# Five gate projections of a hybrid decoder layer, formed as block products by Strassen's scheme with tokens on the partitions

## The chip, the cores and the metric

The kernel runs on one core of a Trainium2 chip. It is one program: TensorE does the matrix products, VectorE and ScalarE the elementwise work, SyncE (SP) issues every DMA, GpSimd does next to nothing. The metric is the device time of one execution in microseconds, the median of three runs. Time before: 1664.78 us (1664.39 to 1664.81).

## What is computed

One layer, 512 tokens (S), width 2048 (D), float32:

```
h    = rmsnorm(x) * (1 + scale) + shift          # shift, scale, gate = silu(c) @ w_ada + b_ada
proj = h @ w_in                                  # 2048 x (768 + 512 + 64 + 6 * 2048)
q_lat, kv_lat, k_rope, z_mla, u, v, z_sgu, g_mla, g_sgu = split(proj)
y_mla = causal_attention(rmsnorm(q_lat) @ w_uq, rmsnorm(kv_lat) @ w_ukv, k_rope) * silu(z_mla)
mixed = tril(w_spatial) @ rmsnorm(v) + b_spatial # per group of 128 channels and chunk of 128 tokens
y_sgu = u * mixed * silu(z_sgu)
out   = rmsnorm(x + gate * ((sigmoid(g_mla) * y_mla + sigmoid(g_sgu) * y_sgu) @ w_out))
```

The five projections that only gate something (z_mla, g_mla, u, z_sgu, g_sgu; in the code z, g, u, s, t) are five products of 512 x 2048 by 2048 x 2048. They are the largest part of the arithmetic.

## The kernel before

**Precision.** Every large product is made of three: each operand is split into a high part in the matmul's float32r type and the low rest, and `mm3` (L133) adds high by high, high by low and low by high in one PSUM bank. Splitting takes a copy on ScalarE and a subtraction on VectorE (`hilo`, L138). Weights are split too: `Stream` (L53) brings a granule of 128 x 1024 numbers by DMA into one of three raw tiles (`dma_to`, L76), copies it to `whi` on ScalarE (L97), subtracts to `wlo` on VectorE (L98), and keeps two such pairs. `get` (L103) hands a granule to the matmuls and first emits the split of the next one and the DMAs behind it.

**Order.** The program runs under a manual schedule: each engine takes its instructions in the order in which the Python code emits them, and waits in place where an operand isn't ready. Small tasks are kept in two lists, `pend` (evacuations of PSUM) and `bg` (background), and a loop pops one between the matmuls of two granules. DMAs stand in one queue (SP) in the order of emission; `load_before` ties a load to the DMA of a granule.

**Stages.**
1. The adaLN products (dot products on VectorE, L125, rows of `wada`) beside the first 1024 columns of the projection (latents), then 640 more (the latent rest, and the last 128 columns of z, g and u). These 1664 columns are computed without the shift, whose share is added later: `shift_share` (L224) multiplies the raw weights, loaded a second time, with the shift on VectorE, `shift_bias` (L599) sums over the partitions.
2. The v columns (L466), tokens on the partitions: h is the stationary operand, 512, 384 or 320 columns of weights move. `evac_v` (L487) copies v into SBUF tiles `b0` to `b15`.
3. The gate stage (L749 to L827). For each of 15 heads (128 columns) and each of the five types: one PSUM bank, two granules, 8 chunks of 128 of the depth each, three matmuls a chunk: weights are stationary, 512 tokens of h move. Channels therefore lie on the partitions. `evac` (L693) multiplies the result into the tiles `g` and `b` of that head, with a sigmoid on ScalarE where it is a silu or a gate; these tiles stay in SBUF until the attention merges them. The last head's s and t follow (L814). Beside it run, from `bg` or at fixed places: the SGU mixing of each pair of groups (`sgu_prep`, `sgu_mix`, L649 to L690), the rotary tables (`rope_part`, L520, 34 small VectorE operations for each of four parts), 32 shares of the shift, and from head 8 on the scaling, squares, roots and norms of the latents (L612 to L717), their splitting (`lat_split`, L795) and the rotary key.
4. The attention, head by head (L1008): projections of q, k and v from the latents, scores, softmax, transposes, value product, merge with the gates.
5. The output projection, residual and final norm (L1068).

PSUM has eight banks, given out in turn by `bank` (L295).

## Time and profile before

| | |
|---|---|
| median of three runs | 1664.78 us |
| the profiled execution | 1664.88 us, span 1663.2 us, granted clock 0.999 |
| busy: TensorE, VectorE, ScalarE, GpSimd | 1651.6, 947.5, 583.3, 2.2 us |
| DMA | 228.6 MB, mean 137 GB/s |

By stages, from the windows of the trace (us):

| stretch | stage | TensorE | VectorE | ScalarE | DMA share |
|---|---|---|---|---|---|
| 0 to 101 | adaLN, first latents | 97.3 | 86.9 | 45.8 | 0.88 |
| 101 to 155 | 640 more columns | 54.0 | 50.6 | 18.5 | 0.84 |
| 155 to 337 | v | 182.0 | 95.8 | 61.8 | 0.55 |
| 337 to 788 | gates, heads 0 to 7, SGU, tables | 451.0 | 246.5 | 135.6 | 0.38 |
| 788 to 1201 | gates, heads 8 to 15, latents | 413.0 | 161.7 | 120.5 | 0.28 |
| 1201 to 1480 | attention | 278.9 | 223.8 | 148.5 | 0.20 |
| 1480 to 1663 | output | 175.3 | 82.2 | 52.8 | 0.38 |

How to read the rows shown below: a group of instructions gives line, engine, operation, what it writes and reads, shapes and count, then busy microseconds and the mean nanoseconds of one, then how long the engine was idle just before them and what it waited for. A row of the timeline gives start, duration, engine, line and operation. Matmuls overlap, so their spacing, not their duration, is the price. PE is TensorE, DVE VectorE, ACT ScalarE, SPq the queue of SP.

### The profile page before, as it was taken

The numbers are of one execution on the slowest core, as the hardware profiler recorded it, in microseconds if no ns is written. First come the engines' busy times: TensorE is split into PE (matmuls) and PEld (weight loads), VectorE is DVE, ScalarE is ACT, GpSimd is POOL, SyncE is SP. The second block draws the span as 40 slices with busy tenths as digits, with TensorE's granted clock in tenths as the row PEclk, the third lists the DMA queues.
The fourth block names the chain that finished last, engine by engine and source line by source line (L and its number), as shares of the span: only waits on it lengthen the run. The fifth ranks groups of instructions, "written<-read, shape, count | busy, mean of one in ns | idle before, by whom it ended". The sixth has DMA issues, their size and how long they took to land.

```text
span 1663.2 us, 20082 instructions
## 1 busy us (share of the span) xinstructions
PE 1651.6 (99%) x8024; PEld 1406.1 (85%) x8024; DVE 947.5 (57%) x1456; ACT 583.3 (35%) x967; POOL 2.2 (0%) x11
## 2 busy tenths in 40 slices
PE   9999999999999999999999999999999999999998
PEld 7888889988888888888888888888898888888887
DVE  8988646365665644444443533323578778874453
ACT  4343333234223322221223322222455555542332
POOL 0000000000000000000000000000000000000000
PEclk9999999999999999999999999999999999999999
DMA  9878557344444333322222222232311221126332
GB/s 379 346 295 303 193 211 269 101 151 143 142 152 132 120 137 127 123 102 89 98 92 102 89 101 100 90 102 81 96 61 58 63 75 55 61 77 253 127 101 101
DMA packets 64508, 228.63 MB, mean 137 GB/s; under 512 B 7304, under 2 KB 9376, under 8 KB 57632
## 3 DMA queue, kind: packets, MB, share of 16 engines
q1 hardware_dynamic: 64416, 227.37, 38.7%
q8 instruction: 62, 1.02, 0.2%
q14 instruction: 30, 0.25, 0.0%
HBM read 223.14 MB, written 4.20 MB: 137 GB/s over the span
## 4 chain that ended last, share of the span: by engine, by line
PE 98%; DMA 1%; DVE 0%; ACT 0%; issue 0%; SPq 0%; DVEq 0%
PE ps L135 32%; PE ps L134 32%; PE ps L136 32%; PE ps L947 1%; PE ps L675 1%; PE ps L910 1%; PE ps L911 1%; DMA wraw<-in_w 1%; PE ps L676 0%; DMA wada<-in_c 0%; PE ps L606 0%; DVE wlo L98 0%; ACT whi L97 0%; PE ps L446 0%; DVE wada L122 0%
## 5 line engine op out<-in xcount | busy, mean ns | idle before, releaser
L98 DVE TENSOR_TENSOR wlo<-wraw,whi 128x1024 fp32r<-128x1024 f32 (+3 forms) x304 | 339.0, 1115 | 577.4 <-ACT whi L97 566.4
L134 PE MATMUL ps<-hh,whi 128*128 128x512 f32 x1640 | 641.6, 391 | 0.2 <-ACT hh L389 0.2
L135 PE MATMUL ps<-hl,whi 128*128 128x512 f32 x1640 | 638.5, 389 | 0.8 <-DVE hl L125 0.8
L136 PE MATMUL ps<-hh,wlo 128*128 128x512 f32 x1640 | 638.4, 389 | 0.0
L97 ACT CAST whi<-wraw 128x1024 fp32r<-128x1024 f32 (+3 forms) x304 | 293.7, 966 | 801.6 <-PE ps L135 561.0
L136 PEld LDWEIGHTS ps<-hh,wlo 128*128 128x128 f32 x1640 | 307.8, 188 | 64.5 <-DVE wlo L98 0.2
L135 PEld LDWEIGHTS ps<-hl,whi 128*128 128x128 f32 x1640 | 308.0, 188 | 64.0 <-DVE hl L125 1.1
L134 PEld LDWEIGHTS ps<-hh,whi 128*128 128x128 f32 x1640 | 307.9, 188 | 63.7 <-ACT hh L389 0.6
L134 PE MATMUL ps<-whi,hh 128*128 128x512 f32 (+3 forms) x448 | 148.9, 332 | 0.0
L135 PE MATMUL ps<-wlo,hh 128*128 128x512 f32 (+3 forms) x448 | 148.6, 332 | 0.1
L136 PE MATMUL ps<-whi,hl 128*128 128x512 f32 (+3 forms) x448 | 148.5, 332 | 0.0
L125 DVE SCALAR_TENSOR_TENSOR wada<-wada,cact 128x2048 f32<-128x2048 f32 x47 | 107.2, 2281 | 1.2 <-DMA wada<-in_wada 1.2
L135 PEld LDWEIGHTS ps<-wlo,hh 128*128 128x128 f32 x448 | 84.6, 189 | 5.4 <-DVE wlo L98 0.4
L136 PEld LDWEIGHTS ps<-whi,hl 128*128 128x128 f32 x448 | 84.6, 189 | 5.0
L134 PEld LDWEIGHTS ps<-whi,hh 128*128 128x128 f32 x448 | 84.6, 189 | 5.0
L134 PE MATMUL ps<-whi,b 128*128 128x512 f32 (+1 forms) x212 | 81.8, 386 | 0.0
L135 PE MATMUL ps<-wlo,b 128*128 128x512 f32 (+1 forms) x212 | 81.6, 385 | 0.0
L136 PE MATMUL ps<-whi,g 128*128 128x512 f32 (+1 forms) x212 | 81.6, 385 | 0.0
L134 PEld LDWEIGHTS ps<-whi,b 128*128 128x128 f32 x212 | 39.8, 188 | 7.9
L135 PEld LDWEIGHTS ps<-wlo,b 128*128 128x128 f32 x212 | 39.8, 188 | 7.9
L136 PEld LDWEIGHTS ps<-whi,g 128*128 128x128 f32 x212 | 39.8, 188 | 7.9
L139 ACT CAST lat<-ps 128x512 fp32r<-128x512 f32 (+1 forms) x64 | 35.4, 570 | 13.4 <-PE ps L136 13.3
(229 smaller groups left out, 1340.8 us busy)
## 6 DMA issues: line engine op xcount, KB each, us to landing
wraw<-in_wh SPq DMA_DIRECT2D x150, 512.0 KB, 3.3
wada<-in_wada SPq DMA_DIRECT2D x47, 1024.0 KB, 5.9
wraw<-in_w SPq DMA_DIRECT2D x32, 512.0 KB, 3.5
wraw<-in_wo SPq DMA_DIRECT2D x32, 512.0 KB, 3.3
wraw<-in_w SPq DMA_DIRECT2D x32, 320.0 KB, 2.9
wraw<-in_wv SPq DMA_DIRECT2D x16, 512.0 KB, 3.2
wraw<-in_wv SPq DMA_DIRECT2D x16, 384.0 KB, 3.3
wraw<-in_wq SPq DMA_DIRECT2D x16, 384.0 KB, 2.9
```

The costliest lines, as they stand in the source:

```text
L97: self.nc.scalar.copy(hi[:, :n], raw[:, :n])
L98: self.nc.vector.tensor_tensor(out=lo[:, :n], in0=raw[:, :n], in1=hi[:, :n].bitcast(F32), op=ALU.subtract)
L125: DVE.scalar_tensor_tensor(out=out, in0=in0, scalar=scalar, in1=in1, op0=op0, op1=op1, **kw)
L134: PE.matmul(ps, ah, bh, start=start, stop=False)
L135: PE.matmul(ps, ah, bl, start=False, stop=False)
L136: PE.matmul(ps, al, bh, start=False, stop=stop)
L139: ACT.copy(hi, src)
L675: PE.matmul(ps[:, n2], vh[:, n, :], whl[:, q], start=True, stop=False)
L910: PE.matmul(ps, q2[:, q], krh[:, :n], start=False, stop=False)
L911: PE.matmul(ps, q2[:, q], krl[:, :n], start=False, stop=True)
L947: PE.transpose(ps[:, o:o + P], pr_[i][:, j * P:(j + 1) * P], ident)
```

## The change

The five projections are cut into ten blocks of twice 512 columns (one of twice 320; z, g and u lack their last 128 columns, as before). In a block the 512 tokens, the depth of 2048 and the columns are halved: h becomes four quarters of 256 x 1024, the weights four of 1024 x 512. Strassen's scheme (in Winograd's form) makes the four quarters of the result from seven products of quarters. Each product has four granules ("items" in the code) of 256 rows of the depth, 12 matmuls each: two chunks, two token tiles, three matmuls. h is stationary, weights move, so tokens lie on the partitions.

Four sums of quarters of h are formed once and kept split: S1, S2 and S4 in new tiles during the v columns, S3 in place of a quarter of h that is no longer needed. The sums of weight quarters are formed anew in each block on VectorE before they are split: a running sum T in the order of the products P1, P6, P2 with P7, P3, P5, P4. Products accumulate in PSUM (banks `y` and `z`, two token tiles each); three intermediate results are copied to SBUF by ScalarE, and the four quarters of the result come from PSUM and these copies.

There is no room to keep results in SBUF, and they have tokens on the partitions. So `gates` loads the step before (z for g, mixed v for u, and so on) from DRAM, multiplies, and stores again; after g and t the tile is transposed on TensorE (`turned`) and stored, and the attention loads it head by head (`fetch`). v, the mixed v, the latents and the rotary key go through DRAM too. The SGU mixing now has the spatial weights stationary and four chunks of v moving, with the bias added by ScalarE. Latent scaling is done during the v columns. `Stream` takes raw tiles and pairs from lists that grow and shrink (three pairs and up to four raw tiles in this stage), may need two loads for a granule or none, and `get` now splits two granules ahead.

The diff, cut to its core:

```diff
+BLOCKS = (
+    ((("z", 0, 512),), (("z", 512, 512),)),
+    ((("z", 1536, 384), ("g", 1024, 128)), (("z", 1024, 512),)),
+    ((("g", 0, 512),), (("g", 512, 512),)),
+    ((("u", 0, 512),), (("u", 512, 512),)),
+    ((("g", 1664, 256), ("u", 1664, 256)), (("g", 1152, 512),)),
+    ((("u", 1024, 320),), (("u", 1344, 320),)),
+    ((("s", 0, 512),), (("s", 512, 512),)),
+    ((("t", 0, 512),), (("t", 512, 512),)),
+    ((("s", 1024, 512),), (("s", 1536, 512),)),
+    ((("t", 1024, 512),), (("t", 1536, 512),)),
+)
...
+            src = form(raws) if form is not None else raws[0][:, :n]
             if to is not None:
                 hi, lo = to()
             else:
-                hi = self.pool.tile([P, GW], F32R, tag="whi", name=f"whi{k}", bufs=self.hl_bufs)
-                lo = self.pool.tile([P, GW], F32R, tag="wlo", name=f"wlo{k}", bufs=self.hl_bufs)
-            self.nc.scalar.copy(hi[:, :n], raw[:, :n])
-            self.nc.vector.tensor_tensor(out=lo[:, :n], in0=raw[:, :n], in1=hi[:, :n].bitcast(F32), op=ALU.subtract)
+                pool, tag = self.parts[self.next_part]
+                self.next_part = (self.next_part + 1) % len(self.parts)
+                hi = pool.tile([P, GW], F32R, tag=tag + "h", name=f"{tag}h_{k}")
+                lo = pool.tile([P, GW], F32R, tag=tag + "l", name=f"{tag}l_{k}")
+            self.nc.scalar.copy(hi[:, :n], src)
+            self.nc.vector.tensor_tensor(out=lo[:, :n], in0=src, in1=hi[:, :n].bitcast(F32), op=ALU.subtract)
             self.hl[k] = (hi, lo)
-        for consume, raw in later:
+            if after is not None:
+                after(raws)
+            if not keep:
+                self.free(k)
+            if frees is not None:
+                self.free(frees)
...
-        self.dma_to(self.n_split - 1 + self.raw_bufs)
+        self.dma_to(self.n_split + 6)
...
+                elif whole:
+                    n = w - (P if c0 + w == D else 0)
+                    src = wh[h:h + n // P, t, kh][:, :, i * 256:(i + 1) * 256].rearrange("h p w -> p h w")
+                    loads.append((lambda x, o=o, n=n: x[:, 2 * o:2 * (o + n)].rearrange("p (h w) -> p h w", w=256), src))
...
+        def first(raws, b=b, i=None, n=n):
+            if T[i] is None or T[i][0] != b:
+                T[i] = (b, nt(c1[0].p, [P, GW], F32, f"T{i}"))
+            tt(T[i][1][:, :n], raws[0][:, :n], raws[1][:, :n], ALU.add)
+        def t_of(raws, i, n=n):
+            return T[i][1][:, :n]
+        def t_add(raws, i, n=n):
+            t = T[i][1][:, :n]
+            tt(t, t, raws[0][:, :n], ALU.add)
+            return t
+        def both(raws, n=n):
+            t = raws[0][:, :n]
+            tt(t, t, raws[1][:, :n], ALU.add)
+            return t
+        kept = {}
+        def hold(raws, i, n=n, kept=kept):
+            kept[i] = raws[0][:, :n]
+            return t_add(raws, i, n)
+        seq = [(1, i) for i in range(4)] + [(6, i) for i in range(4)]
+        seq += [(2, 0), (7, 0), (2, 1), (7, 1), (2, 2), (2, 3), (7, 2), (7, 3)]
+        seq += [(p, i) for p in (3, 5, 4) for i in range(4)]
+        for p, i in seq:
+            if p == 1:
+                e = ws.add((w(0, 0, i), w(0, 1, i)), n, after=lambda raws, f=first, i=i: f(raws, i=i))
+            elif p == 2:
+                e = ws.add(w(1, 1, i), n, form=lambda raws, f=hold, i=i: f(raws, i), keep=True)
+                gc[b, i] = e
+            elif p == 7:
+                e = ws.add((), n, form=lambda raws, kept=kept, i=i: kept.pop(i), frees=gc[b, i])
+            elif p == 3:
+                e = ws.add((w(0, 1, i), w(1, 1, i)), n, form=both)
+            elif p == 5:
+                e = ws.add(w(1, 0, i), n, after=lambda raws, f=t_add, i=i: f(raws, i))
+            else:
+                e = ws.add((), n, form=lambda raws, f=t_of, i=i: f(raws, i))
+            items.append((b, p, i, e))
+            n_item += 1
+            if 4 <= b < 7 and n_share < 2 * KC and n_item % 5 in (1, 3):
...
+    def make_s12(j):
+        a, b = (nt(tb.p, [P, S], F32, f"t{i}") for i in range(2))
+        tt(a, hh[j].bitcast(F32), hl[j].bitcast(F32), ALU.add)
+        tt(b[:, right], hh[j + 8].bitcast(F32)[:, right], hl[j + 8].bitcast(F32)[:, right], ALU.add)
+        tt(b[:, right], a[:, right], b[:, right], ALU.subtract)
+        split_sum("s1", j, b[:, right])
+        tt(b[:, left], b[:, right], a[:, left], ALU.subtract)
+        split_sum("s2", j, b[:, left])
+    def make_s4(j):
+        a, b = (nt(tb.p, [P, S], F32, f"t{i}") for i in range(2))
+        tt(a[:, left], sums["s2h"][:, j].bitcast(F32), sums["s2l"][:, j].bitcast(F32), ALU.add)
+        tt(b[:, left], hh[j + 8].bitcast(F32)[:, left], hl[j + 8].bitcast(F32)[:, left], ALU.add)
+        tt(a[:, left], a[:, left], b[:, left], ALU.add)
+        split_sum("s4", j, a[:, left])
...
+    for i in range(13):
+        early.setdefault(8 + i, []).append(lambda i=i: lat_scale(i))
+    for j in range(8):
+        early.setdefault(11 + 2 * j + j // 2, []).append(lambda j=j: make_s12(j))
+        early.setdefault(32 + j, []).append(lambda j=j: make_s4(j))
...
+    def turned(t, ty, n, c0, w):
+        ps = bank()[:, :w]
+        for q in range(w // P):
+            PE.transpose(ps[:, q * P:(q + 1) * P], t[:, q * P:(q + 1) * P], ident)
+        o = copy_slot()[:, :w]
+        ACT.copy(o, ps)
+        h0 = c0 % 1024 // P
+        DMA.dma_start(out_d[ty][c0 // 1024][h0:h0 + w // P, :, n * P:(n + 1) * P].rearrange("h p w -> p h w"),
+                      o.rearrange("p (h w) -> p h w", w=P))
...
+    def gates(all_):
+        tile_, n, pieces = open_.pop(0)
+        o, turns = 0, []
+        for ty, c0, w in pieces:
+            t, src = tile_[:, o:o + w], all_[:, o:o + w]
+            o += w
+            if ty != "u":
+                s_ = sig()[:, :w]
+                ACT.activation(s_, src, AF.Sigmoid)
+            if ty == "z":
+                tt(t, src, s_, ALU.mult)
+            elif ty == "u":
+                tt(t, src, t, ALU.mult)
+            else:
+                tt(t, t, s_, ALU.mult)
+                if ty == "s":
+                    tt(t, src, t, ALU.mult)
+            if ty in "gt":
+                turns.append((t, ty, n, c0, w))
+            else:
+                DMA.dma_start(piece_of(step_d, ty, n, c0, w), t)
+        if not turns:
+            later(2, open_next)
+            return
+        def turn():
+            for a in turns:
+                turned(*a)
+            later(1, open_next)
+        later(2, turn)
...
+    def result(which, pair, store, n, c, w):
+        def f():
+            ps = pair[n][:, :w]
+            if which == "y":
+                gates(ps)
+                return
+            t = store[n][:, :w]
+            if which == "u2":
+                tt(t, ps, t, ALU.subtract)
+            elif which == "z6":
+                tt(t, t, ps, ALU.subtract)
+            else:
+                tt(t, ps, t, ALU.add)
+            gates(t)
+        return f
...
+    def sgu_group(g):
+        p, q = g // 2, g % 2
+        _, gr_, whl = sgw[p]
+        v = as3(sgw["v"])
+        for n in range(NB):
+            ACT.activation(v[:, n], v[:, n], AF.Copy, scale=rv[:, n:n + 1])
+        tt(v, v, gr_[:, q * P:(q + 1) * P].unsqueeze(1).broadcast_to([P, NB, P]), ALU.mult)
+        vh, vl = slot("cosT", F32R), slot("sinT", F32R)
+        hilo(vh, vl, sgw["v"])
+        if g + 1 < H:
+            v_load(g + 1)
+        if q == 1 and p + 1 < 8:
+            sgu_load(p + 1)
+        def mix():
+            ps = bank()
+            mm3(ps, whl[:, q, :P], whl[:, q, P:], vh, vl, True, True)
+            m = copy_slot()
+            ACT.activation(m, ps, AF.Identity, bias=sgw["b"][:, g:g + 1])
+            DMA.dma_start(tokens(mix_d, slice(g * P, (g + 1) * P)), as3(m))
+        later(2, mix)
...
+    def fetch(h):
+        vt[h] = nt(bp.p, [P, S], F32, f"b{h}")
+        DMA.dma_start(vt[h], out_d["t"][h // 8][h % 8])
+        gt[h] = nt((ga if h < 8 else g2p).p, [P, S], F32, f"g{h}")
+        DMA.dma_start(gt[h], out_d["g"][h // 8][h % 8])
...
+    for idx, (b, p, i, e) in enumerate(items):
+        now[0] = idx
+        w = width(b)
+        at_ = idx % 28
+        last = b == len(BLOCKS) - 1
+        if last and (p, i) == (2, 0):
+            ws.leaving = raw3
+        ending = last and p == 4 and i > 1
+        if ending and i == 3:
+            ws.shrink_parts((c1[0].p, "w2"))
+        wH, wL = ws.get(e, ahead=1 if ending else 2)
...
+            if b == 4:
+                bg.extend([None] * 28)
+            if b == 5:
+                two = [(lambda a=a: [f() for f in a]) for a in (rope[k:k + 2] for k in range(0, len(rope), 2))]
+                bg[:] = [None] * 6 + [rope_begin, None, None, *two]
+            if b == 7:
+                bg.extend(tasks_of_latents())
+                bg.extend([key_load, None, None, key_turn, None, key_rotary])
...
+        pair, lf = (y if p in (1, 2, 3, 4) else z), lefts[p]
+        for k in range(2):
+            for n in range(2):
+                fh, fl = lf(2 * i + k, n)
+                mh_, ml_ = moving(wH, b, k), moving(wL, b, k)
+                ps = pair[n][:, :w]
+                st = i == 0 and k == 0 and p in (1, 5, 6)
+                PE.matmul(ps, fh, mh_, start=st, stop=False, skip_group_check=True)
+                PE.matmul(ps, fh, ml_, start=False, stop=False, skip_group_check=True)
+                PE.matmul(ps, fl, mh_, start=False, stop=i == 3 and k == 1, skip_group_check=True)
+        if i == 3:
+            if p in (1, 2, 6):
+                base = {1: 0, 6: 2, 2: 4}[p]
+                store = [slot(f"lat{base + n}") for n in range(2)]
+                for n in range(2):
+                    ACT.copy(store[n][:, :w], pair[n][:, :w])
+                if p == 1:
+                    p1 = store
+                elif p == 6:
+                    z6 = store
+                else:
+                    u2 = store
+            elif p == 7:
+                evs += [("u2", result("u2", z, u2, n, 1, w)) for n in range(2)]
+            elif p == 3:
+                evs += [("z6", result("z6", y, z6, n, 1, w)) for n in range(2)]
+            elif p == 5:
+                evs += [("p1", result("p1", z, p1, n, 0, w)) for n in range(2)]
+            elif p == 4:
+                evs += [("y", result("y", y, None, n, 0, w)) for n in range(2)]
...
+        until = (4 * 28 - 3, 7 * 28 - 1, 9 * 28 + 14)[0 if b < 4 else 1 if b < 7 else 2]
+        busy = bool(evs)
+        if evs:
+            evs.pop(0)[1]()
+        if bg and (not busy or last or len(bg) * 28 >= (until - idx) * 20):
+            f = bg.pop(0)
+            if f:
+                f()
```

## The prediction

> **What bounds the kernel now.** I read the page first: its busy times and the chain of work that ended last.

> ```profile
> span 1663.2 us, 20082 instructions
> ...
> PE 1651.6 (99%) x8024; PEld 1406.1 (85%) x8024; DVE 947.5 (57%) x1456; ACT 583.3 (35%) x967; POOL 2.2 (0%) x11
> ...
> PE 98%; DMA 1%; DVE 0%; ACT 0%; issue 0%; SPq 0%; DVEq 0%
> ```

> TensorE is the chain; the others hide behind it. Then the busy time by stretches: the start, three of the v columns, the gate stage with heads 0 to 7 (337 to 788), the rest of it with the first projections behind it, and the last 13 us.

> ```profile
> core 0: us, PE busy (x) PEld busy (x) DVE busy (x) ACT busy (x) POOL busy (x), PEclk, DMA share, GB/s
> 0.00:101.00 101.00, 97.30 (x485) 80.89 (x486) 86.93 (x115) 45.75 (x65) 2.19 (x11) 1.00 0.88 345
> ...
> 155.00:242.00 87.00, 87.00 (x386) 72.03 (x385) 51.46 (x56) 29.47 (x53) 0.00 (x0) 1.00 0.57 209
> 242.00:309.00 67.00, 67.00 (x389) 67.00 (x388) 37.32 (x36) 22.41 (x61) 0.00 (x0) 1.00 0.61 216
> 309.00:337.00 28.00, 28.00 (x192) 27.96 (x191) 7.01 (x8) 9.87 (x29) 0.00 (x0) 1.00 0.33 107
> 337.00:788.00 451.00, 451.00 (x2057) 375.58 (x2056) 246.51 (x412) 135.56 (x181) 0.00 (x0) 1.00 0.38 130
> 788.00:1200.00 412.00, 412.00 (x1824) 341.25 (x1823) 160.67 (x181) 119.96 (x149) 0.00 (x0) 1.00 0.28 94
> ...
> 1650.00:1663.00 13.00, 5.33 (x45) 5.12 (x43) 3.40 (x11) 2.44 (x7) 0.00 (x0) 0.88 0.29 108
> ```

> In the gate stage TensorE never rests, VectorE is busy 407 of 863 us and the DMA engines 28 to 38%. So fewer matmuls shorten this stage one for one, as long as what feeds them keeps up. VectorE is the feeder to watch.

> **What TensorE gains.** Starts of the first and last matmul of a head (240 of them), of a 320-wide column group of v (192), of one SGU pair's sixteen matmuls and the next one, and ten transposes in the chain:

> ```profile
> 473.02 0.45 PE L134 MATMUL ps<-hh,whi 128*128 128x512 f32 x1
> 527.28 0.39 PE L136 MATMUL ps<-hh,wlo 128*128 128x512 f32 x1
> ...
> 308.52 0.31 PE L134 MATMUL ps<-whi,hh 128*128 128x320 f32 x1
> 336.52 0.31 PE L136 MATMUL ps<-whi,hl 128*128 128x320 f32 x1
> ...
> 358.46 0.28 PE L675 MATMUL ps<-whl,vh 128*128 128x256 f32 x1
> 360.25 0.45 PE L134 MATMUL ps<-hh,whi 128*128 128x512 f32 x1
> ...
> 1221.11 1.09 PE ps L947 x10
> ```

> A 512-wide matmul takes 54.26/239 = 0.227 us, a 320-wide one with tokens stationary 28.00/191 = 0.147, a transpose 0.109, an SGU pair 1.79. Before: 77 column tiles x 16 chunks x 3 = 3696 matmuls, 839.0 us, and 8 pairs, 14.3: 853.3. After: ten blocks x 7 products x 4 granules x 12 = 336 matmuls a block; nine blocks of 76.3 and one (the sixth, block 5) of 49.3, together 736.0. SGU: 16 x 3 x 0.227 = 10.9. New transposes, for g and t only: 15 and 16 heads x 4 token tiles = 124, 13.5. Together 760.4, and 0.7 for six odd transposes. **TensorE alone: -92.2 us.**

> **What VectorE must do for it.** A block forms 28 hi/lo pairs, 280 in the stage where there were 150 and eight of half size, and each pair costs ScalarE a copy and VectorE a subtraction; sixteen sums of weight quarters (after P1, before P2 and P3, after P5) go to VectorE too, and fourteen 512-wide result and gate operations. Prices: groups by line and shape, then starts on VectorE, and a copy with the subtraction that follows it:

> ```profile
> L98 DVE TENSOR_TENSOR wlo<-wraw,whi 128x1024 fp32r<-128x1024 f32 x216 | 264.5, 1225 | 505.9 <-ACT whi L97 495.8 <-PE ps L676 9.7
> L97 ACT CAST whi<-wraw 128x1024 fp32r<-128x1024 f32 x216 | 227.7, 1054 | 690.4 <-PE ps L135 526.4 <-PE ps L136 89.0 <-issue 54.3
> L98 DVE TENSOR_TENSOR wlo<-wraw,whi 128x640 fp32r<-128x640 f32 x24 | 19.8, 824 | 24.6 <-ACT whi L97 24.3
> L97 ACT CAST whi<-wraw 128x640 fp32r<-128x640 f32 x24 | 17.5, 727 | 49.1 <-PE ps L136 19.6 <-PE ps L135 19.5 <-issue 10.0
> L125 DVE SCALAR_TENSOR_TENSOR acc<-wraw,shift,acc 128x1024 f32<-128x1024 f32 x15 | 19.2, 1279 | 0.0
> L125 DVE SCALAR_TENSOR_TENSOR acc<-wraw,shift,acc 128x640 f32<-128x640 f32 x15 | 13.2, 879 | 0.0
> L215 DVE RECIPROCAL rq<-rq 128x512 f32<-128x512 f32 x1 | 3.4, 3354 | 0.7 <-ACT rq L214 0.7
> ...
> 62.61 1.23 DVE L98 TENSOR_TENSOR wlo<-wraw,whi 128x1024 fp32r<-128x1024 f32 x1 [0.43 <-ACT whi L97]
> 63.76 0.75 DVE L125 SCALAR_TENSOR_TENSOR hl<-x,gxA,hh 128x512 fp32r<-128x512 f32 x1
> ...
> 353.60 0.69 DVE L122 TENSOR_TENSOR g<-ps,sig 128x512 f32<-128x512 f32 x1 [0.69 <-ACT sig L697]
> ...
> 369.18 0.22 DVE L129 TENSOR_SCALAR rd<-rb 128x128 f32<-128x128 f32 x1
> 370.02 0.29 DVE L122 TENSOR_TENSOR rs<-rs,rd 128x128 f32<-128x128 f32 x1
> ...
> 397.58 0.42 DVE L122 TENSOR_TENSOR wsr<-wsr,tri 128x256 f32<-128x256 f32 x1
> 398.48 0.42 DVE L122 TENSOR_TENSOR whl<-wsr,whl 128x256 fp32r<-128x256 f32 x1 [0.47 <-ACT whl L139]
> 398.82 0.68 DVE L122 TENSOR_TENSOR b<-b,rv 128x512 f32<-128x512 f32 x1
> 400.19 0.69 DVE L122 TENSOR_TENSOR vl<-b,vh 128x512 fp32r<-128x512 f32 x1 [0.69 <-ACT vh L139]
> 400.80 0.68 DVE L122 TENSOR_TENSOR b<-b,rv 128x512 f32<-128x512 f32 x1
> ```

> Start to start, a 1024-wide operation holds VectorE 1.15 us (62.61 to 63.76), a 512-wide one 0.61 (400.19 to 400.80), a 640-wide one 0.75 (824 ns less the same overlap). A 512-wide block: 44 x 1.15 + 14 x 0.61 = 59.1 us; with eight more gate operations in an s block, 64.0. The 320-wide block: 44 x 0.75 + 14 x 0.4 = 38.6.

> In these queues an instruction waits in order, so waits count as well. In P2 and P3 a sum feeds the copy and the copy the subtraction: VectorE stands for 1.23 + 1.05 + 0.06 of handing over less 1.15 = 1.19 us, eight times a block, 9.5. A sigmoid between two operations leaves 0.69 idle (353.60), six times, 4.1; it also delays the next granule's copy, by 1.05 - 0.65 = 0.4, eight times, 3.2. So with waits a block takes 75.9 (z, g, t), 80.8 (s) and 68.6 (u, without sigmoid); the 320-wide one 38.6 + 8 x 0.85 = 45.4.

> Background work, popped between granules on the same queues:
> - Blocks 0 to 3: eight token sums of P3 at 0.61 + 0.42 + 0.47 + 0.35 = 1.85 (pure 1.31); sixteen SGU groups at 1.98 (398.82 to 400.80) and 0.4 for the delayed copy, 38.1 (pure 16 x 1.22); eight spatial weights at 1.24 (397.58 to 398.82), 9.9 (pure 6.7).
> - Blocks 4 to 6: 32 shares of the shift, 16 x 1.20 + 16 x 0.88 (the 640 now in two pieces) = 33.3, a third a block; rotary tables, 34 small operations x 4 parts x 0.28 (four from 369.18 to 370.31) = 38, in blocks 5 and 6.
> - Blocks 7 to 9: four reduces, ten squares, two reciprocals of 3.35, ten norms, ten splits: 32; 12 more for waits on roots and swaps, an estimate.

> | blocks | TensorE | VectorE pure | with waits |
> |---|---|---|---|
> | 0-3 | 320.0 | 273 | 359 |
> | 4 | 78.9 | 70 | 87 |
> | 5, 6 | 125.6 | 163 | 186 |
> | 7-9 | 235.9 | 214 | 277 |
> | sum | 760.4 | | 909 |

> Only blocks 5 and 6 exceed TensorE without any wait, by 37 us. For the other rows the bound below is TensorE's time, above the column with waits. I take the latter: VectorE may run only two granules ahead (three pairs of hi/lo tiles), so slack cannot be saved up. P1 and P6 leave some; P3 and P5 do not: their eight granules and four evacuations take 4 x 3.49 + 4 x 2.30 + 4 x (1.91 + 0.4) = 32 us against 21.8 of matmuls. Before, evacuations stood behind ten granules of a head, now behind 28 shorter ones with the sums among them.

> **The rest.** Latent scaling (13 x 0.61) and the sums of h move into the v columns: S1 and S2 8 x 3.3, S4 8 x 1.85, 49 us. The rows above show 96 of 182 us used, so they fit, but next to a 2.3 us dot in one granule of 4.2; 0 to 8, I take 3. Results go through DRAM: per block eight loads and eight stores of up to 256 KB, and 32 loads in the attention; the idle two thirds of the DMA engines hide them. SP issues some 45 DMAs a block, 19 us of 76 at the 0.43 quoted below; stores stand in its queue ahead of weight loads and wait for VectorE, which is late anyway. Seven PSUM banks instead of eight in the attention I cost at nothing: if a bank is late there, the same heads show TensorE idle.

> Weight quarters arrive in 1 KB pieces (512 B and less in block 5), which before's weights never do. Nearest rows, landing times and two issues on SP:

> ```profile
> wraw<-in_wh SPq DMA_DIRECT2D x150, 512.0 KB, 3.3
> wsr<-in_wsT SPq DMA_DIRECT2D x8, 128.0 KB, 3.2
> bsr<-in_bsp SPq DMA_DIRECT2D x8, 128.0 KB, 4.5
> ...
> 468.52 0.43 SPq L640 DMA_DIRECT2D wsr<-in_wsT  x1
> 469.00 0.42 SPq L642 DMA_DIRECT2D bsr<-in_bsp  x1
> ```

> bsr (512 B pieces) is issued 0.48 us behind wsr and lands 0.48 + 4.5 - 3.2 = 1.78 us after it: at least 74 GB/s. The gate stage moves 94 GB/s at a share of 0.28 in 4 KB pieces: 336 GB/s. A block needs 24 loads of 0.52 MB and 4.2 MB of results, 16.8 MB: 50 us at 336, under its 76; at 74 for the loads, 183. The bsr row holds waiting too, so I take the upper rate, no cost, and keep the other as a rival. [...]

> **Sum.** The profiled execution took 1664.9 us (span 1663.2 and 1.7 around it), 0.1 above the median of the runs. 1664.9 - 853.3 + 909 + 0.7 + 3 = **1725 us**. Own range 1690 to 1760.

> **Rivals.**
> - VectorE's waits are absorbed outside blocks 5 and 6: **faster**. For: in the first 101 us VectorE is busy 86.9, TensorE 97.3. Against: there one granule brings one subtraction, here bursts of sums and evacuations. With all waits gone 1664.9 - 853.3 + 798 + 0.7 = 1610; with a part left 1630. It decides where the waits outside those two blocks cost under 28 us of the 88 counted: TensorE's 635 there, 186 for the two, and 4 for the rest, against 853.
> - The DMA engines set the pace: 1 KB pieces near the 512 B price. A line through 111 ns for 512 B (16 pieces on each of 16 engines in 1.78 us) and 195 ns for 4 KB (336 GB/s) gives 123 ns for 1 KB, 133 GB/s: 95 us a block for weights and, at 2 KB, 19 for results. Ten blocks, 1100 with the narrow one: about 1910. Against: bsr is one source row for all partitions, and waits behind wsr.
> - TensorE's clock falls in the gaps. In the last 13 us TensorE is busy 5.3 and the clock is 0.88. [...]
> - No change: the waits cost just those 28 us.

> **Chances.** Forecast 0.57; absorbed waits 0.27; DMA pace 0.13; no change 0.03. A difference under 0.2% (3.3 us) cannot be told from none in this kernel. Faster 0.27, same 0.03, slower 0.70. The range, 1620 to 1800, leaves out the DMA case and the best of the absorbed ones.

> **What would show it.** TensorE busy near 90%, VectorE near 1300 us (947 - 407 + the pure column's 720 + 49); TensorE's waits named after the subtraction of the hi/lo pair, largest in blocks 5 and 6, and in P3 and P5 of the others; 336 matmuls in 76 us only in P1 and P6. Wrong, if TensorE waits for raw loads, or if blocks 0 to 3 and 7 to 9 run at 76 to 80 us.

## The result, and the profile after

The changed kernel takes 1906.18 us (median; 1901.08 to 1906.4), the kernel before 1664.63 us beside it: a ratio of 1.144, 95% interval 1.142 to 1.146. The forecast was 1725 us, with 1620 to 1800 as its range. "Slower" was right; the time is 106 us beyond the upper end.

The page of the changed kernel: its span, busy times, granted clock in tenths by slices, DMA packets, and the chain of work that ended last.

```profile
span 1904.1 us, 21254 instructions
...
PE 1685.2 (89%) x7738; PEld 1386.0 (73%) x7738; DVE 1320.0 (69%) x1866; ACT 775.2 (41%) x1244; POOL 3.1 (0%) x11
...
PEclk9999999989989999988889799988989999999999
DMA packets 249912, 342.40 MB, mean 180 GB/s; under 512 B 22808, under 2 KB 191312, under 8 KB 243024
...
PE 51%; DVE 19%; DMA 14%; ACT 9%; issue 4%; SPq 2%; ACTq 0%; DVEq 0%
```

TensorE was 98% of the chain and is 51% of it now. The granted clock of TensorE is 7 or 8 tenths in 10 of the 40 slices of 47.6 us, all of them within the gate stage.

Busy times by stretches of the changed kernel (columns as in the prediction): a part of the v columns, the gate stage, the attention with the output.

```profile
242.00:309.00 67.00, 63.40 (x350) 61.92 (x349) 51.95 (x74) 24.56 (x51) 0.00 (x0) 0.97 0.78 267
...
343.00:1431.00 1088.00, 884.07 (x3554) 687.56 (x3553) 736.24 (x906) 432.94 (x611) 0.00 (x0) 0.91 0.58 179
1431.00:1890.00 459.00, 458.50 (x2461) 398.19 (x2460) 307.53 (x586) 206.86 (x413) 0.00 (x0) 1.00 0.34 113
```

The gate stage begins at 343.1 us, 6.4 us later than before; what follows it takes 473.0 us (1904.1 - 1431.1), as before (1663.2 - 1190.0 = 473.2). So the loss is the gate stage: 1088.0 us against 853.3 before and 760.4 of TensorE's work by the prediction's count. The 327.6 us above that count are of two kinds: TensorE is idle for 203.9 us, and it is busy for 884.1 - 760.4 = 123.7 us more than the count, at a granted clock of 0.91.

Three of the ten blocks in the same view (blocks 3, 5 and 6), and then block 1 phase by phase (P1, P6, P2 with P7, P3, P5, P4):

```profile
668.67:765.85 97.18, 86.92 (x357) 67.46 (x356) 67.57 (x69) 43.75 (x63) 0.00 (x0) 0.96 0.65 199
...
881.92:973.80 91.88, 64.66 (x341) 57.62 (x340) 64.86 (x136) 24.21 (x39) 0.00 (x0) 0.87 0.60 173
973.80:1102.61 128.81, 98.33 (x339) 71.68 (x337) 93.95 (x162) 39.60 (x49) 0.00 (x0) 0.87 0.50 158
```

```profile
461.75:479.85 18.10, 13.52 (x53) 10.46 (x52) 11.96 (x12) 7.98 (x13) 0.00 (x0) 0.91 0.81 255
479.85:491.45 11.60, 11.60 (x53) 9.61 (x52) 7.00 (x7) 7.59 (x13) 0.00 (x0) 1.00 0.29 93
491.45:517.55 26.10, 24.63 (x104) 18.75 (x102) 16.84 (x19) 13.42 (x23) 0.00 (x0) 1.00 0.44 129
517.55:536.75 19.20, 13.87 (x50) 9.94 (x49) 12.79 (x14) 6.85 (x9) 0.00 (x0) 0.91 0.84 256
536.75:556.80 20.05, 15.18 (x53) 11.34 (x52) 14.06 (x16) 8.14 (x14) 0.00 (x0) 0.83 0.57 174
556.80:567.88 11.08, 11.08 (x52) 9.05 (x51) 8.33 (x11) 6.18 (x11) 0.00 (x0) 1.00 0.19 53
```

A phase of four granules is 48 matmuls, 10.9 us. P6 and P4, which load nothing, come close to that. P1 and P3, which load two quarters for each granule, take 18.1 and 19.2 us; P5 with one load and a sum takes 20.1. VectorE is busy for only 66% of P1, and the DMA engines for 0.81: neither is full where TensorE waits.

What TensorE waited for in the gate stage (total us, times, longest; L1233 to L1235 are the three matmuls of a product, L786 the transposes of g and t, L202 the first of the SGU's three matmuls), and what SyncE's queue stood for before it issued DMAs (L127 issues what `Stream` loads, weight quarters for the most part):

```profile
PE ps L786 <- DVE lat L190: 48.8, 22, 9.2
PE ps L1233 <- ACT w2h L158: 28.8, 14, 5.2
PE ps L1233 <- ACT w0h L158: 24.0, 10, 4.3
PE ps L202 <- ACT cosT L207: 19.7, 9, 4.6
PE ps L1234 <- DVE w2l L159: 19.1, 24, 2.6
```

```profile
SPq L127 <- DVE T L190: 127.1, 53, 4.9
SPq L127 <- DVE w0l L159: 100.7, 21, 20.1
SPq L127 <- DVE w2l L159: 98.0, 22, 12.5
SPq L127 <- DVE w1l L159: 74.4, 18, 15.4
```

In these four rows the loads stand for 400.2 us until VectorE has finished with the raw tile that they are to fill; not all of that delays TensorE. The next lines are the chain of waits in a window over P1 of block 1 (start, length, what). They show what one such turn takes, and, ahead of it, matmuls at 0.43 us apiece:

```profile
445.78 0.43 PE ps L204
...
450.47 0.30 PE ps L1234
450.77 0.23 PE ps L1235
...
464.19 0.38 SPq L127
464.57 0.04 issue
464.61 5.21 DMA wraw<-in_wh
...
469.92 1.05 ACT w2h L158
470.97 0.02 issue
470.99 1.23 DVE w2l L159
472.22 1.14 DVE T L190
```

From the issue of the load (464.19) to the end of the sum that frees the tile (473.36) a raw tile is held for 9.2 us. The stage has four raw tiles, and a granule of P1 takes two. So two granules pass in 9.2 us, and four in 18.4: P1 measured 18.1 here, and 18.6 in the mean of the ten blocks. This is arithmetic on one turn; the runs below test it.

### The profile page after: what moved, and what is told of

The parts are those of the page before. It is cut to its first block, busy times and chain, and to the rows that moved or that the text cites. A ratio compares the mean times of both kernels' runs of the same rounds, so it can differ in the third digit from the quotient of the medians.

```text
span 1904.1 us, 21254 instructions
## 1 busy us (share of the span) xinstructions
PE 1685.2 (89%) x7738; PEld 1386.0 (73%) x7738; DVE 1320.0 (69%) x1866; ACT 775.2 (41%) x1244; POOL 3.1 (0%) x11
## 4 chain that ended last, share of the span: by engine, by line
PE 51%; DVE 19%; DMA 14%; ACT 9%; issue 4%; SPq 2%; ACTq 0%; DVEq 0%
PE ps L203 13%; PE ps L204 13%; PE ps L202 13%; DMA wraw<-in_wh 10%; DVE T L190 4%; PE ps L1234 4%; PE ps L1235 3%; PE ps L1233 3%; DVE w2l L159 3%; DVE lat L190 3%; DVE w0l L159 2%; ACT w1h L158 2%; ACT w0h L158 2%; ACT w2h L158 2%; DVE w1l L159 2%
## 5 line engine op out<-in xcount | busy, mean ns | idle before, releaser
L159 DVE TENSOR_TENSOR w0l<-wraw,w0h 128x1024 fp32r<-128x1024 f32 (+2 forms) x127 | 142.2, 1119 | 94.3 <-ACT w0h L158 93.5
L159 DVE TENSOR_TENSOR w1l<-wraw,w1h 128x1024 fp32r<-128x1024 f32 (+3 forms) x127 | 135.6, 1068 | 99.7 <-ACT w1h L158 98.7
L158 ACT CAST w0h<-wraw 128x1024 fp32r<-128x1024 f32 (+2 forms) x127 | 123.0, 968 | 191.5 <-DVE wraw L190 46.6
L158 ACT CAST w1h<-wraw 128x1024 fp32r<-128x1024 f32 (+3 forms) x127 | 117.3, 924 | 178.1 <-PE ps L204 43.6
L1233 PE MATMUL ps<-w2h,hh 128*128 128x512 f32 (+1 forms) x212 | 94.5, 446 | 25.5 <-ACT w2h L158 25.5
L1233 PE MATMUL ps<-w0h,hh 128*128 128x512 f32 (+1 forms) x216 | 92.8, 429 | 21.5 <-ACT w0h L158 21.5
L1234 PE MATMUL ps<-w2l,hh 128*128 128x512 f32 (+1 forms) x212 | 93.7, 442 | 11.9 <-DVE w2l L159 11.9
L1234 PE MATMUL ps<-w0l,hh 128*128 128x512 f32 (+1 forms) x216 | 92.9, 430 | 12.5 <-DVE w0l L159 12.5
L1233 PE MATMUL ps<-w1h,hh 128*128 128x512 f32 (+1 forms) x212 | 89.2, 421 | 10.6 <-ACT w1h L158 10.6
L190 DVE TENSOR_TENSOR T<-T,wraw 128x1024 f32<-128x1024 f32 (+1 forms) x80 | 94.3, 1178 | 1.5 <-DMA wraw<-in_wh 1.5
L202 PE MATMUL ps<-w0h,hh 128*128 128x256 f32 (+3 forms) x288 | 92.9, 323 | 1.0 <-ACT w0h L158 1.0
L1235 PE MATMUL ps<-w2h,hl 128*128 128x512 f32 (+1 forms) x212 | 91.1, 430 | 0.0
L1235 PE MATMUL ps<-w0h,hl 128*128 128x512 f32 (+1 forms) x216 | 90.4, 419 | 0.0
L202 PE MATMUL ps<-hh,w1h 128*128 128x512 f32 x218 | 86.7, 398 | 0.0
L1235 PE MATMUL ps<-w1h,hl 128*128 128x512 f32 (+1 forms) x212 | 86.4, 407 | 0.0
## 6 DMA issues: line engine op xcount, KB each, us to landing
wraw<-in_wh SPq DMA_DIRECT2D x168, 512.0 KB, 5.0
wraw<-in_w SPq DMA_DIRECT2D x32, 512.0 KB, 5.6
wraw<-in_wo SPq DMA_DIRECT2D x32, 512.0 KB, 3.6
wraw<-in_wh SPq DMA_DIRECT2D x88, 128.0 KB, 3.4
wraw<-in_wv SPq DMA_DIRECT2D x16, 512.0 KB, 4.3
```

The lines of the kernel that those rows point to most:

```text
L158: self.nc.scalar.copy(hi[:, :n], src)
L159: self.nc.vector.tensor_tensor(out=lo[:, :n], in0=src, in1=hi[:, :n].bitcast(F32), op=ALU.subtract)
L190: DVE.tensor_tensor(out=out, in0=in0, in1=in1, op=op)
L202: PE.matmul(ps, ah, bh, start=start, stop=False)
L1233: PE.matmul(ps, fh, mh_, start=st, stop=False, skip_group_check=True)
L1234: PE.matmul(ps, fh, ml_, start=False, stop=False, skip_group_check=True)
```

## Experiments

The theory after the result: the turn of the raw tiles sets P1 and P3. Its rivals: the DMA engines' rate on 1 KB pieces (the second rival of the prediction, whose 1910 us lies 4 us from the result); VectorE's work as such; the trip of the gate results through DRAM; the SGU's place in TensorE's order. All times below are medians, and differences are to the changed kernel's 1906.2 us unless another is named. "Stage" is the gate stage.

### Pieces of 4 KB instead of 1 KB

```diff
+        return wh[(b + 2 * i + 8 * ch) % (H - 1), b % 5, kh][:, :2 * width(b)]
         loads, o, whole = [], 0, width(b) % P == 0
```

> Each weight quarter of the gate stage is read as one run of 4 KB per partition (2.5 KB in the narrow block) from another place of the same tensor, in as many loads and bytes as before: the quarters are then not the right ones. The rest is unchanged. Theory 'VectorE' (its queue, with what it waits for in order, sets the pace of the gate stage, as predicted): loads are early anyway, 1890 to 1910 us. Theory 'loads' (weight quarters land late because they come in pieces of 1 KB and less; raw loads are 10% of the chain of waits, some 190 us): 1750 to 1830 us, landing time down from 5.0 to about 3.3 us. Theory 'order' (TensorE stands in its own queue in front of transposes and SGU matmuls whose inputs VectorE has just been given): 1880 to 1910 us.

The edit also merges loads where a quarter comes from two types or has the narrow width, 240 loads in place of 336, so they are not "as many".

Measured: 1866.97 us, ratio to before 1.122 (1.118 to 1.125), so -39 us. A load in 1 KB pieces landed 5.0 us after its issue, in 4 KB pieces 4.5 (first the changed kernel, then this one; operation, count, size, median to landing):

```profile
wraw<-in_wh SPq DMA_DIRECT2D x168, 512.0 KB, 5.0
```

```profile
wraw<-in_wh SPq DMA_DIRECT2D x216, 512.0 KB, 4.5
```

The pieces cost something, but five sixths of the 241 us lost stay; the result lies in none of the three ranges. The rival of the DMA pace would have given back most of the loss.

### One load for a granule of P1 and P3

P1's sum adds the loaded quarter to itself, P3's adds T to the one loaded; VectorE's work is unchanged.

```diff
-                e = ws.add((w(0, 0, i), w(0, 1, i)), n, after=...)
+                e = ws.add(w(0, 0, i), n, after=...)
-                e = ws.add((w(0, 1, i), w(1, 1, i)), n, form=both)
+                e = ws.add(w(1, 1, i), n, form=...)
```

> P1 and P3 load one weight quarter per granule instead of two (16 loads a block instead of 24); the second term of their sums is taken from SBUF, so that VectorE, ScalarE and TensorE have the same instructions, and the weights of P1's and P3's sums are not the right ones. Theory 'raw loop' (four raw tiles: a tile is free 3.5 us after its data is there, and the next data lands 5 us after that, 8.5 us for two granules that need two tiles each and last 5.4): P1 and P3 fall from 17 to 21 us in the ordinary blocks to 11 to 14, the whole to 1740 to 1800 us. Theory 'VectorE': its queue has the same work, 1880 to 1905 us.

Measured: 1791.51 us, ratio 1.076 (1.073 to 1.079), -115 us, as the raw loop had it; P1 falls to 13.9 us in the mean of the blocks, P3 only to 17.9. This takes away loads and halves the tiles of a granule at once, so it needs the next run.

### Seven raw tiles instead of four

The four T tiles become one, and their room holds three raw tiles more. Loads, pieces and operations stay. The one T tile also makes a sum wait for the readers of the sum before it; what that costs was not measured.

```diff
-            if T[i] is None or T[i][0] != b:
-                T[i] = (b, nt(c1[0].p, [P, GW], F32, f"T{i}"))
+            if T[0] is None:
+                T[:] = [(b, nt(c1[0].p, [P, GW], F32, "T0"))] * 4
...
     ws.grow(part=(c1[0].p, "w2"))
+    extra = [(c1[0].p, f"wraw{k}") for k in (4, 5, 6)]
+    for r in extra:
+        ws.grow(raw=r)
```

> The four tiles of running weight sums become one, so the sums are not the right ones, but each operation stays; the room goes to three more raw tiles, seven in all. Loads, bytes and all work are as before. Theory 'raw loop': P1 falls to 11 to 14 us and P3 to 14 to 16 (there the sum, the copy and the subtraction follow each other, 3.5 us a granule), the whole to 1750 to 1810 us. Theory 'VectorE': 1885 to 1910 us. If instead the rate of the DMA engines for 1 KB pieces is what lacks: 1860 to 1890 us, with landing times over 6 us.

Measured: 1810.60 us, ratio 1.088 (1.085 to 1.091), -96 us. The gate stage and the loads of this kernel:

```profile
340.50:1333.50 993.00, 848.80 (x3554) 664.82 (x3554) 733.88 (x906) 431.45 (x611) 0.00 (x0) 0.95 0.64 196
```

The stage is 95 us shorter with the same bytes in the same pieces, and VectorE as busy as before (733.9 against 736.2). With seven tiles, two granules of P1 would need 9.2 x 4 / 7 = 5.3 us by their turn, under the 5.5 of their matmuls. P1 falls from 18.6 to 13.8 us in the mean, where 11 to 14 was expected. P3 falls from 22.6 to 19.6 only, where 14 to 16 was expected, so the turn of the tiles is not the only limit there. The DMA engines had the rate to give: 196 GB/s at a busy share of 0.64, against 179 at 0.58.

### Seven raw tiles and 4 KB pieces

Both edits above together.

> Seven raw tiles as above and 4 KB rows together. Theory 'raw loop': shorter landing adds little where there are tiles enough, 1730 to 1800 us; then what is left is VectorE's queue and the order, and the forecast's own sum of 1725 us is near. Theory 'VectorE': 1850 to 1870 us, what the rows alone gave.

Measured: 1800.49 us, ratio 1.082 (1.079 to 1.085). That is at the upper end of what the raw loop had, and far from the forecast's 1725. With the tiles in place the pieces are worth 10 us, a quarter of the 39 above: what they cost was mostly the longer turn. This kernel's gate stage, 76 us above the 909 that the forecast has for it:

```profile
340.88:1326.20 985.32, 848.43 (x3554) 665.44 (x3553) 733.20 (x906) 431.40 (x611) 0.00 (x0) 0.95 0.60 197
```

TensorE is idle 136.9 us; the prediction's waits were 909 - 760.4 = 148.6. Beside them it is busy 88.0 us beyond the count. In the kept trace the clock is at half for 102.4 us of this stage, and TensorE busy for 95.0 of them; a matmul then takes 0.43 us instead of 0.227, so some 45 us of the 88 are the clock, for which the forecast's sum has no term. The other 43, by what is left over, are short waits that the overlapping records show as busy.

### Without the weight sums

The sixteen sums of a block are left out; copies and subtractions stay.

```diff
-            tt(T[i][1][:, :n], raws[0][:, :n], raws[1][:, :n], ALU.add)
...
-            t = T[i][1][:, :n]
-            tt(t, t, raws[0][:, :n], ALU.add)
-            return t
+            return raws[0][:, :n]
...
-            t = raws[0][:, :n]
-            tt(t, t, raws[1][:, :n], ALU.add)
-            return t
+            return raws[0][:, :n]
```

> The sixteen sums of weight quarters of every block are left out; each product takes one of its two quarters, or a sum formed once, so that the loads, the pairs and the matmuls stay as they are. VectorE loses 156 sums of 1.15 us, 180 us, and the wait between sum, copy and subtraction in P2 and P3. Theory 'VectorE': the gate stage falls from 1088 us to 800 to 860, the whole to 1620 to 1680 us. Theory 'loads': raw tiles become free a microsecond sooner, no more, 1830 to 1890 us. Theory 'order': the waits of TensorE on transposes and SGU shrink with VectorE's lag, 1780 to 1850 us.

Measured: 1759.20 us, ratio 1.057 (1.053 to 1.061), -147 us: no theory's range holds it. The sums are a part of the tile's turn and of VectorE's queue at once, so the same was tried where tiles are not short:

### Seven raw tiles, 4 KB pieces, no sums

> Seven raw tiles, 4 KB rows and no weight sums: TensorE's floor is 1573 us. If VectorE's sums and late loads together make the loss, 1600 to 1650 us, faster than before. If the order of TensorE's queue, evacuations and background hold a share of their own, 1680 to 1730 us.

Measured: 1663.16 us, ratio 0.999 (0.997 to 1.000). Against the run with the sums (1800.5) that is -137 us, and against the run without sums on four tiles (1759.2) it is -96. So the two costs nearly add: some 140 us for the sums in VectorE's queue, some 100 for tiles and pieces, whichever goes first. The time lies between the two ranges expected. The mean length of three phases over the ten blocks (us, start to start in the timelines) shows where each edit acts:

| kernel | P1 | P3 | P5 |
|---|---|---|---|
| changed | 18.6 | 22.6 | 16.3 |
| 4 KB pieces | 17.7 | 21.1 | 15.6 |
| seven tiles | 13.8 | 19.6 | 14.3 |
| seven tiles, 4 KB | 13.7 | 18.2 | 15.4 |
| no sums | 15.8 | 15.6 | 15.4 |
| seven tiles, 4 KB, no sums | 12.3 | 12.1 | 12.8 |
| matmuls alone | 10.5 | 10.5 | 10.5 |

In P1 the turn of the tiles gives the length of three kernels on four tiles to within 3%: 18.4 us, 17.4 with a landing 0.5 shorter, 16.1 without the sum's 1.14. In P3 tiles and sums both bind, and in P5 little is gained until both go.

The stage of this kernel, and its waits (the profiled execution is its fastest, 1656.5 us):

```profile
339.82:1182.10 842.28, 792.29 (x3554) 643.75 (x3553) 561.05 (x747) 433.02 (x611) 0.00 (x0) 0.99 0.69 231
```

```profile
PE ps L1234 <- DVE w1l L159: 14.4, 13, 3.7
...
PE ps L786 <- DVE lat L190: 1.8, 3, 0.8
```

The transposes (L786), which cost TensorE 48.8 us of waiting for gate products and 34.0 with seven tiles and 4 KB pieces, now wait 1.8. The trip through DRAM is still there, so it was late products of VectorE, and not DRAM, that they waited for. Even so the kernel only draws level with the one before. TensorE is idle for 50.0 us and busy 31.9 beyond its count, some 10 of them by the clock (half for 23.9 us); the longest blocks, from the start of their first product to that of the next block's, are 0, 6, 8 and 9 (93.7, 88.9, 98.7 and, to its own end, 89.7 us), where background work lies beside the products. What each piece of it costs was not tried.

### Seven raw tiles, no sums, 1 KB pieces

> The changed kernel with seven raw tiles (one T tile in place of four) and without the sixteen weight sums of each block, which are left out (the products run on unsummed quarters); the quarters are read in their 1 KB pieces. It stands beside the kernel with seven tiles, no sums and 4 KB rows (1663 us). Theory, the pieces cost a longer landing and no rate: with enough tiles they cost what they cost beside the sums, 10 us, so about 1673 us. Rival, the pieces cost DMA rate, hidden so far behind VectorE: the step without sums asks faster for its quarters, and at least the 39 us of the run with four tiles comes out, 1700 us or more.

Measured: 1681.53 us, ratio 1.010 (1.009 to 1.012): the pieces cost 18 us here, between the 10 and the 39 of the two expectations. Its gate stage:

```profile
341.68:1206.30 864.62, 803.74 (x3554) 652.59 (x3553) 561.36 (x747) 432.86 (x611) 0.00 (x0) 0.97 0.72 225
```

All loads and results of the stage, in the pieces of the changed kernel, passed in 865 us. The rival of the DMA pace needed 1100. It is refuted, though its total came close to the result. Bytes over busy share say the same: 179 / 0.58 = 309 GB/s in the changed kernel's stage, and 225 / 0.72 = 312 here against 231 / 0.69 = 335 with 4 KB pieces, where that rival had 133.

### Without the results' trip through DRAM

The results are neither loaded, stored nor transposed in the gate stage.

```diff
-            if ty == "u":
-                DMA.dma_start(t[:, o:o + w], mix_d[n][:, c0:c0 + w])
-            elif ty != "z":
-                DMA.dma_start(t[:, o:o + w], piece_of(step_d, before[ty], n, c0, w))
...
-            if ty in "gt":
-                turns.append((t, ty, n, c0, w))
-            else:
-                DMA.dma_start(piece_of(step_d, ty, n, c0, w), t)
```

> The gate results are formed with as many VectorE and ScalarE operations, but not loaded from, nor stored to DRAM, and g and t are not transposed; the attention reads another tensor of the same size in their place. Theory 'VectorE': its work is the same, 1880 to 1900 us. Theory 'loads': a quarter of the block's bytes goes, and no store stands in SP's queue ahead of a weight load, 1780 to 1850 us. Theory 'order': the 49 us for which TensorE waits in front of transposes go, with the slow clock behind them, 1810 to 1850 us.

Measured: 1875.25 us, ratio 1.127 (1.123 to 1.130), -31 us, of which the 13.5 us of the transposes themselves are a part; it lies just below the range of 'VectorE' and above the two others. The same edit with seven tiles, 4 KB pieces and no sums:

> Seven raw tiles, 4 KB rows, no sums, and the gate results are not loaded, stored or transposed between the blocks (the gates are formed from tiles that are there, the attention reads x transposed). It stands beside the same kernel with the trip through DRAM (1663 us, of which 62 us are TensorE's waits in the gate stage and 27 us its half-clock matmuls). Theory, the waits left are those of the transposes and of VectorE's gate products: about the 31 us that leaving the trip out gave in the changed kernel itself, 1632 us. Rival, they come from the work laid into the gate stage beside the blocks (the SGU's matmuls, the shares, the evictions), which this run keeps: within 10 us of 1663 us.

Measured: 1640.93 us, ratio 0.986 (0.984 to 0.987), -22 us against the kernel with the trip (1663.2). Less the 13.5 us of transposes, the trip costs 9 us there. The run lies between its two expectations. (The waits in the trace of the kernel with the trip come to 50 us and its half-clock matmuls to some 10, not to the 62 and 27 named above.)

### The mixed v two granules later

```diff
-        later(2, mix)
+        later(4, mix)
```

> The three SGU matmuls of a group are issued four granules after its operands were ordered, instead of two; nothing else changes. Theory 'order': the 22 us for which TensorE waits in front of them (nine waits, up to 4.6 us) go, and half-clock matmuls behind them, 1860 to 1885 us. Theories 'VectorE' and 'loads': what TensorE does not wait for here it waits for at the next granule, 1895 to 1910 us.

Measured: 1898.09 us, ratio 1.140 (1.137 to 1.144), -8 us, within the range of 'VectorE' and 'loads'; the interval still touches that of the changed kernel (1.142 to 1.146). TensorE's waits at L202 (19.7 us in the changed kernel) went, but the granules behind them waited longer, and its idle time in the stage is 205.2 us against 203.9: idle time only moved along the queue.

### T's sums on GpSimd

Seven raw tiles and 4 KB pieces; twelve of the sixteen sums are made by another engine.

```diff
-            tt(T[i][1][:, :n], raws[0][:, :n], raws[1][:, :n], ALU.add)
+            nc.gpsimd.tensor_tensor(T[i][1][:, :n], raws[0][:, :n], raws[1][:, :n], ALU.add)
...
-            tt(t, t, raws[0][:, :n], ALU.add)
+            nc.gpsimd.tensor_tensor(t, t, raws[0][:, :n], ALU.add)
```

> Seven raw tiles and 4 KB rows, all sums made, but the twelve of each block that P1, P2 and P5 make into T are on GpSimd instead of VectorE (T is one tile and the rows read are other ones, so the numbers computed differ from the reference; the work is the same). It stands between the kernel with all sums on VectorE (1800 us) and the one with none (1663 us). Theory, VectorE's time for the sums is what costs: three quarters of 137 us go, about 1697 us, and VectorE is busy about 120 us less than in the run with all sums on it. Rival, the order costs and not the engine (the raw tile is held until the sum is made, wherever it is made, and the products of P4 wait for T): a GpSimd sum slower than VectorE's 1.15 us holds the tiles longer, 1800 us or more.

Measured: 1867.14 us, ratio 1.121 (1.119 to 1.123): 67 us slower than with the sums on VectorE (1800.5). Groups of instructions with the sums on GpSimd (busy us, mean ns):

```profile
L380 POOL TENSOR_TENSOR T<-T,wraw 128x1024 f32<-128x1024 f32 (+1 forms) x80 | 217.8, 2722 | 470.6 <-DMA wraw<-in_wh 219.7 <-DVE w2l L159 97.7 <-DVE w0l L159 66.9
...
L190 DVE TENSOR_TENSOR lat<-lat,lat 128x512 f32<-128x512 f32 (+4 forms) x122 | 94.4, 776 | 39.2 <-ACT lat L806 32.0 <-ACT lat L792 2.1 <-DMA lat<-u_d 1.2
L190 DVE TENSOR_TENSOR lat<-ps,lat 128x512 fp32r<-128x512 f32 (+4 forms) x102 | 66.9, 664 | 10.1 <-ACT lat L207 9.3 <-PE ps L1239 0.7
```

And with all sums on VectorE:

```profile
L190 DVE TENSOR_TENSOR T<-T,wraw 128x1024 f32<-128x1024 f32 (+1 forms) x80 | 94.4, 1179 | 0.4
L190 DVE TENSOR_TENSOR lat<-ps,lat 128x512 fp32r<-128x512 f32 (+4 forms) x102 | 67.1, 666 | 13.1 <-ACT lat L207 9.3 <-PE ps L1239 3.7
L190 DVE TENSOR_TENSOR lat<-lat,lat 128x512 f32<-128x512 f32 (+4 forms) x122 | 66.6, 549 | 38.2 <-ACT lat L806 33.8 <-DMA lat<-z_d 2.0 <-DMA lat<-s_d 0.3
```

A sum takes 2.72 us on GpSimd against 1.18, so the raw tile is held longer, as the rival said. And VectorE is not relieved: busy 1340.1 us with 120 operations fewer, against 1317.0. Its operations on two SBUF tiles became slower (549 to 776 ns), those with one operand in PSUM did not (666 and 664), with GpSimd busy for 330.7 us; neither expectation held that. How the 67 us divide between this and the longer turn was not tried.

## Why the prediction was right or wrong

**TensorE's saving: right.** P6 and P4 of block 1, at 11.6 and 11.1 us for 10.9 counted, show the matmuls at their forecast cost. The 92 us are there, and nothing of them reaches the end.

**VectorE's work: right.** Forecast "near 1300 us", measured 1320.0; in the gate stage 736 for the pure column's 720. TensorE's share was forecast near 90% and is 89%, but that is luck: the forecast's busy time was 1651.6 - 92.2 = 1559 us, and 1685 were measured.

**The v columns and the attention: right.** 6.4 us for a term of 3 (0 to 8); the attention's seven PSUM banks cost nothing that shows.

**The step that failed first is "I take the upper rate, no cost".** The prediction set bytes against a rate (50 us of transfers under a block of 76) and never set the raw tiles against their turn. That term is 9.2 us x 2 / 4 tiles = 4.6 us a granule in P1, where the matmuls take 2.73. The same omission stands in "P1 and P6 leave some": P6 does, but P1, which the prediction counted as slack, takes 17 to 21 us in the blocks of 512. Measured price: 95 us of stage by the seven tiles, 8 more by the pieces (993.0 to 985.3). "Wrong, if TensorE waits for raw loads" named the sign of it, though TensorE's own rows name the copies and subtractions that wait in turn for loads and sums.

**The clock was left out of the sum.** The 909 us forecast for the gate stage have no term for it, and the length of a single gap does not tell when it falls (last section). Measured: 123.7 us of extra busy time in the stage. The clock is at half for 194.6 us of it, with TensorE busy for 164.8; at some 0.43 us a matmul instead of 0.227 that is about 77 us. The rest, by what is left over, is waits that the overlapping records show as busy. Blocks 5 and 6 have a granted clock of 0.87, block 3 of 0.96. With seven tiles and 4 KB pieces about 45 us of clock remain.

**The waits were near in size, and short.** Forecast were 148.6 us of waiting over the stage. Where tiles and pieces do not bind, 136.9 are idle and some 43 more lie inside the busy time, about 180. So the forecast's 909 goes over into the measurement as 760.4 of matmuls, 180 of waits, 45 of clock and 102.7 of tiles and pieces, 1088 us, and the whole as 1664.9 - 853.3 + 1088.0 + 6.4 = 1906.0. The 180 and the 45 are read from the kernel with seven tiles and 4 KB pieces; in the changed kernel itself the waits of the tiles bring slow matmuls of their own. By rows of the prediction's table, that kernel takes 399 us in blocks 0 to 3 (forecast 359), 91 in block 4 (87), 187 in 5 and 6 (186) and 308 in 7 to 9 (277): blocks 4 to 6 come out as forecast, and nearly all of the 76 us that are missing lie in the first and the last row.

**The DRAM trip, which "the idle two thirds of the DMA engines hide": wrong by some 9 to 18 us,** the 22 and 31 us of the two runs less 13.5 us of transposes. The transposes hang on VectorE's gate products in TensorE's order, as the fall of their waits without the sums shows; how much of the rest is transfers was not separated. That wait was not among the rivals.

**Where the waits would show: half right.** They were to be "named after the subtraction of the hi/lo pair". The largest is the transposes' wait for gate products (48.8 us), then the waits for ScalarE's copies (28.8 and 24.0); the largest of the subtractions' is 19.1. The copies of weight quarters, in turn, stand for VectorE's sums (213 us in the stage) and for raw loads (110). P3 and P5 are among the slow phases, as forecast, and block 6 is the slowest; that P1 is as slow was not forecast.

**The rivals.** "DMA engines set the pace" had the time and not the cause, as the 865 us of the run with 1 KB pieces show. "VectorE's waits are absorbed" (faster) needed waits under 28 us outside blocks 5 and 6; even with sums, tiles and pieces out of the way the stage stands 82 us above its matmuls, 58 of them outside these blocks. That 1 KB pieces cost nothing, as the forecast had it, no run shows. By bytes over busy share, the kernels on seven tiles without sums moved 312 GB/s with them and 335 with 4 KB pieces (the narrow block's pieces under 512 B are among the former). On four tiles such loads landed 0.5 us later (5.0 us against 4.5). They cost most where tiles were few: 39 us on four tiles and 10 on seven, with the sums.

No variant that does the whole work was faster than the kernel before. What stays open is the division of the last 82 us of the stage (842.3 against 760.4): some 9 are the DRAM trip and some 10 the clock, and the background work is a likely part of the rest that no run separates.

## What to carry to other kernels

Before a stage is given loads in place of arithmetic, multiply the turn of a landing tile (issue, landing, and every use until it is free; 9.2 us here) by the tiles that a step takes, divide by the tiles that there are, and set that against the step's own time: that the DMA engines were busy for only 0.58 of the gate stage said nothing about it. Work taken from TensorE and given to the engine that feeds it was paid twice here, by the waits and by the clock that fell with them: a saving of a tenth of the matmuls had to survive some 225 us of both even with tiles enough, about 45 of them the clock. And an alternative that gives the right total is not thereby the cause; one run that keeps its cause and changes something else tells.

## What the runs showed of the hardware that was not expected

```profile
363.44 0.50 PE L1233 MATMUL ps<-w2h,s1h 128*128 128x512 f32 x1 [1.67 <-ACT w2h L158]
364.70 0.50 PE L1234 MATMUL ps<-w2l,s1h 128*128 128x512 f32 x1 [0.76 <-DVE w2l L159]
...
365.37 0.63 PE L1233 MATMUL ps<-w2h,s1h 128*128 128x512 f32 x1
365.80 0.63 PE L1234 MATMUL ps<-w2l,s1h 128*128 128x512 f32 x1
```

After pauses of 1.67 and 0.76 us the matmuls start 0.43 us apart (365.37 to 365.80). In block 8, after pauses of 1.71 and 0.84 us ahead of the matmuls at 1242.29 and 1243.62, they start 0.23 us apart (1243.96 to 1244.19). What goes with the fall shows in five neighbouring windows of 3.41 us. All changes in this trace's 82 clock records lie on one grid of that step (columns as above: TensorE's busy time first, its clock behind the other engines):

```profile
354.92:358.33 3.41, 1.38 (x5) 0.95 (x6) 1.65 (x2) 1.21 (x2) 0.00 (x0) 1.00 0.92 246
358.33:361.74 3.41, 3.41 (x9) 2.15 (x7) 2.25 (x3) 1.30 (x6) 0.00 (x0) 0.50 0.68 213
361.74:365.15 3.41, 0.98 (x4) 0.59 (x4) 1.82 (x4) 1.95 (x4) 0.00 (x0) 1.00 0.62 192
365.15:368.57 3.42, 3.42 (x10) 2.64 (x9) 2.36 (x5) 2.14 (x4) 0.00 (x0) 0.50 0.74 234
368.57:371.98 3.41, 3.41 (x15) 2.44 (x14) 2.38 (x5) 1.54 (x3) 0.00 (x0) 1.00 0.23 77
```

A window in which TensorE was busy for 1.38 or 0.98 us is followed by one at half clock, a full one by full clock. Over the whole stage, laid out on the same grid, 39 windows at full clock are followed by half: TensorE was busy for at most 53% of each. In the 223 followed by full clock it was busy for at least 46%. Of the 57 at half clock, the 18 followed by another such had it busy for at most 85%, the 39 others for at least 81%. So in this stage TensorE's busy share of a window goes with the clock of the next, and the length of one gap does not tell; of the windows at full clock that were busy for 46 to 53%, some were followed by half and some by full.

VectorE took longer on two operands in SBUF in the kernel with twelve sums a block on GpSimd: 776 ns in the mean for its operations on two `lat` tiles, against 549 with all sums on VectorE, with GpSimd busy for 18% of the span, and no change (664, 666) where one operand is in PSUM. Whether each of them was slow just while GpSimd worked was not shown.
